# Lacing the block merges of a triangular inverse with pieces of three projections, with raw buffers of their own for the modulation weights and one transpose for the gathered diagonal blocks

## The chip, the cores and the metric

One Trainium2 chip, one core. The time is device microseconds of one execution of the whole program. Three runs of the kernel before gave 1310.15, 1297.49 and 1303.28 us, a median of 1303.28 us. The engines are called PE (matmul), DVE, ACT, POOL and SP (which issues the transfers).

## The reference, cut to what matters

Two layers (DEPTH 2) over 256 context tokens and 256 latent tokens of width 1024. Each layer has a token mixer and an MLP. The mixer has eight neighbourhood attention heads of width 64 and four gated DeltaNet heads of width 128, which run in both directions. In the DeltaNet heads the reference forms, for every chunk of 64 tokens,

```
a = where(strict, (kb @ k^T) * decay, 0)        # strictly lower triangular
tinv = unit_lower_inverse(a)                    # (I + a)^-1
u = tinv @ (v * beta) ;  w = tinv @ (kb * eg)
```

and then scans the chunks in order with `u`, `w` and the state. The attention heads need the projections `nq`, `nk`, `nv`, and the gated norm needs `z`; none of these depends on the inverse. The modulation vectors (six of width 1024 a layer, from `silu(c) @ w_ada`) are needed at the layer norms, at the end of the mixer and in the MLP.

## The kernel before, in words

All arithmetic is in fp32. A large weight block of 128 x 1024 is fetched by SP into a raw buffer (`wraw`, line 236, a ring of four), split by ACT into a rounded high part (`whi`, line 248) and by DVE into the rest (`wlo`, line 250); both rings have three buffers. A projection is eight steps over the contraction, each of three matmuls of 128 x 512 (`mm3`, lines 274 to 276), 24 in all; the function `getw` hands the weights out in a fixed list order, and up to three blocks are fetched ahead.

The program is written as one long stream, and a scheduler turns it into a queue for each engine: at each moment of its own simulated time it gives an engine the earliest written instruction that is ready there. It does not model the TensorE clock. Work written later fills gaps of work written earlier, as far as its data, its buffers and its PSUM banks allow. Inside a `manual_schedule` region the TensorE instructions of the region keep their written order among themselves; others may still be put between them.

The mixer of a layer (function `mixer`) goes as follows.

- Four DeltaNet heads (`gdn_head`), then the gates (`gates1`, `gates2`).
- For each of four token tiles t, the products `kk` (line 813), the decays (`decay`, ACT exponentials, line 805) and the product of both (line 816) fill 8 of the 32 matrices of 128 x 128 in `U`. Each matrix has four diagonal blocks of 32 x 32.
- The 128 diagonal blocks are inverted together on DVE: line 824 transposes them from `U` to `MT`, line 825 negates them into `Y`, 30 pairs of DVE operations (lines 831 and 833, here called the substitution) run over them, line 834 transposes the result to `MT`, line 836 spreads it over `XT` by four ACT copies, one for each quadrant of 32 partitions, and line 838 spreads its transpose over `U` by four DVE transposes.
- The merges, lines 841 to 872, put the blocks of 32 together to blocks of 64, and those to blocks of 128, in two halves `t2` of 16 matrices. Of each half: 32 matmuls `p1` (line 849), copies to `y1`, 64 matmuls `pz` (lines 853, 854), copies back into `U` and `XT`; then for each of two tiles 8 matmuls `p2` (line 862), a copy to `y2`, 8 matmuls `p3` (lines 867, 868) and the copies back.
- The scan over the chunks (`scan_step`, `o_stage`), written behind the merges.
- Behind that, the string of the layer after its X says in which order the remaining work is written (`run_order`): f is two steps of the modulation (`fill`; one step is one 512 KB block of `w_ada`, line 299, and four small matmuls, line 301), N, K, Q and Z are projections, a is an attention of two heads for one token tile (`attend`). The layer before the X has the heads H and the gates B and C. There are 32 steps of modulation weights and four closing steps in a mixer.

The modulation weights go through the same ring `wraw` as the large weights.

Of the kernel before, what the change touches and what calls it, by code (L numbers as in the profile page):

```python
# [11 lines left out]
F32 = mybir.dt.float32  # L12
# [3 lines left out]
AF = mybir.ActivationFunctionType  # L16
# [6 lines left out]
KT = 8  # L23
# [6 lines left out]
NEG = -1e30  # L30

NHOLD = 6
NB0 = 3
GATE = [("w1t", 0), ("w1", 1, 0)]
PARTS = 4
# [2 lines left out]
PAIR2 = True  # L38
KP_OUT = (2, 3, 0, 1)
CFG = {  # L40
    "ord0": "HHBHHCXfNffffNNfffffNKQffaaaKaQfaaKfaQfaffaaKfaQfaZaaaZZfffafffZ",
    "ord1": "BHHHHCNfffXNfffNfNfKfQfaafKfQfaaKfQKfaQfaafffZZZaZ", "tr": 7, "tr2": 2, "acc": 2, "g": 3, "n": 3,
    "late": 3, "tord": (0, 1, 2, 3), "adab": "n", "depth": 3, "npre": 8, "pre1": (0, 2, 3), "vt": "n",
    "tm": 1, "tmh": (2, 3), "gt": 2, "f02": 1, "f12": 2, "f13": 1,
    "start": "WLmmmWme01WLmmmm2eLmbm0mmbLe1m2m0mme12012bb", "cin": 7, "rows": 1,
# [131 lines left out]
def body(ctx, tc, a, out, dump=None):  # L177
# [289 lines left out]
    def mixer(l, hT, pre, ctx_m):  # L467
# [110 lines left out]
        nv = M.tile([128, 4, 8, 65], F32, name="nv", tag="nv")  # L578
        G.memset(nv[:, :, :, 64:65], 1.0)

        def proj_nv(hp):
            w = getw("w_vz", l, 0, hp)
            ps = proj_T(w, 0, "psv")
# [146 lines left out]

        biases = {}

        def proj_qk(hp, kind):
            if not kind:
                biases[hp] = load_bias(hp)
            w = getw("w_na", l, 2 * hp + kind)
            t0 = 256 if (last and kind) else 0
            ps = proj_T(w, t0, "psn")
# [28 lines left out]

        cnt2 = dict.fromkeys("NKQZaH", 0)

        def run_order(o):  # L770
            for c in o:
                if c in "fBC":
                    {"f": fill, "B": gates1, "C": gates2}[c]()
                    continue
                i = cnt2[c]
                cnt2[c] += 1
# [20 lines left out]
        def decay(t, d, form, bias):  # L797
# [8 lines left out]
                             scale=-1.0 if form == "c" else 1.0)  # L806
            return D_

        for t in ts:
# [10 lines left out]
        q4 = [slice(32 * b, 32 * b + 32) for b in range(4)]  # L820
        MY = M.tile([128, 2, 32, 32], F32, name="MY", tag="my")
        MT, Y = MY[:, 0], MY[:, 1]
# [18 lines left out]
        for t2 in range(2):  # L841
            n0 = 16 * t2
            y1 = tr("y1").rearrange("p (n c) -> p n c", n=16)
            p1 = sm("p1").rearrange("p (n c) -> p n c", n=16)
            pz = sm("pz").rearrange("p (n c) -> p n c", n=16)
            A_, B_ = [slice(64 * r, 64 * r + 32) for r in range(2)], [slice(64 * r + 32, 64 * r + 64) for r in range(2)]
            for r in range(2):
                for n in range(16):
                    PE.matmul(p1[B_[r], n], U[A_[r], n0 + n, B_[r]], XT[A_[r], n0 + n, A_[r]], start=True, stop=True)
                S.activation(y1[B_[r]], p1[B_[r]], AF.Copy)  # L850
            for r in range(2):
                for n in range(16):
                    PE.matmul(pz[A_[r], n], y1[B_[r], n], U[B_[r], n0 + n, B_[r]], start=True, stop=True)
                    PE.matmul(pz[B_[r], n], U[B_[r], n0 + n, B_[r]], y1[B_[r], n], start=True, stop=True)
                V.tensor_scalar(U[A_[r], n0:n0 + 16, B_[r]], pz[A_[r]], -1.0, None, op0=ALU.mult)
                S.activation(XT[B_[r], n0:n0 + 16, A_[r]], pz[B_[r]], AF.Copy, scale=-1.0)
            lo_, hi_ = slice(0, 64), slice(64, 128)
            for t in (2 * t2, 2 * t2 + 1):
                n0 = 8 * t
                p2 = sm("p2").rearrange("p (n c) -> p n c", n=8)  # L860
                for n in range(8):
                    PE.matmul(p2[hi_, n], U[lo_, n0 + n, hi_], XT[lo_, n0 + n, lo_], start=True, stop=True)
                y2 = tr("y2").rearrange("p (n c) -> p n c", n=8)
                S.activation(y2[hi_], p2[hi_], AF.Copy)
                p3 = sm("p3").rearrange("p (n c) -> p n c", n=8)
                for n in range(4):
                    PE.matmul(p3[lo_, n], y2[hi_, n], U[hi_, n0 + n, hi_], start=True, stop=True)
                    PE.matmul(p3[hi_, 4 + n], U[hi_, n0 + 4 + n, hi_], y2[hi_, 4 + n], start=True, stop=True)
                V.tensor_scalar(U[lo_, n0:n0 + 4, hi_], p3[lo_, 0:4], -1.0, None, op0=ALU.mult)
                S.activation(XT[hi_, n0 + 4:n0 + 8, lo_], p3[hi_, 4:8], AF.Copy, scale=-1.0)  # L870
                V.tensor_tensor(U[:, n0 + 4:n0 + 8], XT[:, n0 + 4:n0 + 8],
                                beta[:, t, 4:8].unsqueeze(2).to_broadcast([128, 4, 128]), op=ALU.mult)
        if l == 0:
            dump("LT", U)

        Sst = {t: XT[:, 8 * t:8 * t + 8].rearrange("p (d h) c -> p h d c", d=2) for t in ts}
        vn, on = {}, {}
# [89 lines left out]
        for step in range(4):  # L967
            for d in range(2):
                scan_step(step, d)
        obt = M.tile([128, 16, 2, 64], F32, name="ob", tag="my")  # L970
        run_order(post)
        while steps:
# [340 lines left out]
```

## Time and profile before

| what | before |
| --- | --- |
| median of three runs | 1303.28 us |
| the profiled execution | 1304.05 us, its span 1302.3 us |
| PE busy | 1234.8 us, 95% of the span |
| DVE busy | 875.1 us, 67% |
| ACT busy | 604.6 us, 46% |
| mean granted TensorE clock | 0.963 |
| bytes read from HBM | 187.46 MB, 146 GB/s |

PE is busy nearly all the time, but a busy PE is one that holds a matmul, at whichever clock it was granted. The mean clock of 0.963 therefore belongs to the reading: a stretch at 0.50 does half the work of a stretch at 1.00 while it looks as busy. Times in the sections below are microseconds from the start of the span; the first layer's mixer lies before 330, the second one's between 780 and 1060.

### The profile page before, as it was taken

How to read it: one execution, taken by the hardware profiler on the slowest of the kernel's cores; microseconds unless marked ns; L12 is line 12 of the kernel's file. 1: busy time of each engine (PE TensorE's matmuls, PEld its weight loads, DVE VectorE, ACT ScalarE, POOL GpSimd, SP SyncE). 2: the span in 40 equal slices, each digit the busy share in tenths (PEclk: the TensorE clock that was granted, in tenths of full speed). 3: DMA queues.
4: the chain of work that ended last, by engine and by line, in shares of the span. 5: the costliest groups of instructions: out<-in, count | busy, mean ns of one | idle time of the engine just before them, and what ended most of it. 6: DMA issues, size and time to landing. Idle time of an engine off the chain costs nothing.

```text
span 1302.3 us, 20475 instructions
## 1 busy us (share of the span) xinstructions
PE 1234.8 (95%) x7976; PEld 1006.3 (77%) x7976; DVE 875.1 (67%) x1681; ACT 604.6 (46%) x1079; POOL 81.6 (6%) x82
## 2 busy tenths in 40 slices
PE   7999998999999999999999999899979998999997
PEld 3676666988878988777788888675669877788996
DVE  3788695466579955344444488897965668866677
ACT  2554545565555732322322455555454655544552
POOL 0212100001001000000000001221000010000000
PEclk9999995899999999999999999999958999899999
DMA  9613661023255643533532256235720256555552
GB/s 329 213 65 102 211 219 46 17 78 117 79 194 182 225 150 109 165 130 115 164 129 99 97 178 204 72 107 191 235 92 14 85 179 231 199 184 191 186 187 98
DMA packets 62721, 190.93 MB, mean 147 GB/s; under 512 B 7808, under 2 KB 17824, under 8 KB 62624
## 3 DMA queue, kind: packets, MB, share of 16 engines
q1 hardware_dynamic: 62624, 189.62, 44.2%
q8 instruction: 63, 1.03, 0.3%
q14 instruction: 34, 0.28, 0.1%
HBM read 187.46 MB, written 2.13 MB: 146 GB/s over the span
## 4 chain that ended last, share of the span: by engine, by line
PE 71%; DVE 11%; ACT 4%; issue 2%; POOL 1%; DMA 1%; DVEq 0%; ACTq 0%; POOLq 0%
PE pst L274 7%; PE pst L276 7%; PE pst L275 7%; PE pm L274 7%; PE pm L276 7%; PE pm L275 7%; PE pss L716 3%; PE adaps L301 2%; DVE wlo L250 2%; PE pss L696 2%; PE pss L713 2%; PE psn L274 1%; PE psn L275 1%; PE psn L276 1%; ACT XT L836 1%
## 5 line engine op out<-in xcount | busy, mean ns | idle before, releaser
L250 DVE TENSOR_TENSOR wlo<-wraw,whi 128x1024 fp32r<-128x1024 f32 x224 | 274.7, 1228 | 184.7 <-ACT whi L248 184.3
L248 ACT ACTIVATE whi<-wraw 128x1024 fp32r<-128x1024 f32 x224 | 237.0, 1060 | 316.6 <-PE pst L276 168.9
L274 PE MATMUL pm<-hhi,whi 128*128 128x256 f32 (+1 forms) x544 | 176.4, 324 | 0.8 <-ACT whi L248 0.7
L276 PE MATMUL pm<-hhi,wlo 128*128 128x256 f32 (+1 forms) x544 | 174.5, 321 | 0.0
L275 PE MATMUL pm<-hlo,whi 128*128 128x256 f32 (+1 forms) x544 | 174.4, 321 | 0.0
L274 PE MATMUL pst<-whi,ah 128*128 128x512 f32 x384 | 150.0, 391 | 0.0
L275 PE MATMUL pst<-wlo,ah 128*128 128x512 f32 x384 | 149.5, 389 | 0.0
L276 PE MATMUL pst<-whi,al 128*128 128x512 f32 x384 | 149.1, 389 | 0.0
L274 PEld LDWEIGHTS pm<-hhi,whi 128*128 128x128 f32 x544 | 103.5, 190 | 14.4 <-issue 5.8
L276 PEld LDWEIGHTS pm<-hhi,wlo 128*128 128x128 f32 x544 | 103.6, 190 | 7.7
L275 PEld LDWEIGHTS pm<-hlo,whi 128*128 128x128 f32 x544 | 103.6, 190 | 7.3
L274 PEld LDWEIGHTS pst<-whi,ah 128*128 128x128 f32 x384 | 72.1, 188 | 15.6 <-issue 0.8
L276 PEld LDWEIGHTS pst<-whi,al 128*128 128x128 f32 x384 | 72.1, 188 | 14.8
L275 PEld LDWEIGHTS pst<-wlo,ah 128*128 128x128 f32 x384 | 72.1, 188 | 14.7
L274 PE MATMUL psg<-hhi,whi 128*128 128x512 f32 (+1 forms) x216 | 78.2, 363 | 4.6 <-ACT XT L529 2.3
L276 PE MATMUL psg<-hhi,wlo 128*128 128x512 f32 (+1 forms) x216 | 78.0, 362 | 0.2 <-DVE wlo L250 0.2
L275 PE MATMUL psg<-hlo,whi 128*128 128x512 f32 (+1 forms) x216 | 77.8, 361 | 0.0
L531 DVE SCALAR_TENSOR_TENSOR XT<-U,cw,XT 128x512 f32<-128x512 f32 (+1 forms) x96 | 66.9, 728 | 0.5 <-ACT XT L529 0.4
L1191 ACT ACTIVATE ah<-mr 128x256 fp32r<-128x256 f32 (+1 forms) x68 | 33.5, 492 | 65.6 <-DVE mr L1189 65.6
L301 PE MATMUL adaps<-wraw,scT 128*32 128x256 f32 x640 | 56.0, 397 | 4.8 <-DMA wraw<-w_ada 4.6
L229 POOL TENSOR_TENSOR rs<-ve,mh 128x1 f32<-128x1 f32 x12 | 12.5, 1044 | 629.3 <-DVE bmv L394 362.2
L1192 DVE TENSOR_TENSOR al<-mr,ah 128x256 fp32r<-128x256 f32 (+1 forms) x68 | 35.2, 518 | 24.3 <-ACT ah L1191 24.2
(659 smaller groups left out, 2467.4 us busy)
## 6 DMA issues: line engine op xcount, KB each, us to landing
wraw<-w SPq DMA_DIRECT2D x140, 512.0 KB
wraw<-w_ada SPq DMA_DIRECT2D x80, 512.0 KB
wraw<-w_gdn SPq DMA_DIRECT2D x27, 512.0 KB
wraw<-w_out SPq DMA_DIRECT2D x24, 512.0 KB
xa<-w_ada SPq DMA_DIRECT2D x32, 256.0 KB
wraw<-w_vz SPq DMA_DIRECT2D x16, 512.0 KB
wraw<-w_na SPq DMA_DIRECT2D x16, 512.0 KB
lnrow<-lnr SPq DMA_DIRECT2D x8, 512.0 KB
```

Source lines behind the costliest of these rows:

```text
L248: S.activation(hi, r, AF.Copy)
L250: V.tensor_tensor(lo, r, hi.bitcast(F32), op=ALU.subtract)
L274: PE.matmul(o, l[0], r[0], start=start, stop=False)
L275: PE.matmul(o, l[0], r[1], start=False, stop=False)
L276: last_mm[:] = [PE.matmul(o, l[1], r[0], start=False, stop=stop).ins]
L301: PE.matmul(st["ps"][32 * g:32 * g + 32, :256], scT[:, k, :], w[:, 256 * g:256 * g + 256], start=(k == 0), stop=(k == 7), tile_position=(0 ...
L531: V.scalar_tensor_tensor(av, cin[:, sg:, kk:kk + 256], cw[:, b, kk:kk + 1], av, op0=ALU.mult, op1=ALU.add)
L696: PE.matmul(ps[:, :128 * nkt], nqT[hp][:, a2, qs], nkT[hp][i][:, a2, :128 * nkt], start=i == 0, stop=i == 1)
L713: PE.transpose(ps[:, 128 * kt_:128 * kt_ + 128], p_[:, 128 * kt_:128 * kt_ + 128], ident)
L716: PE.matmul(ps[:, 0:65], p_[:, 128 * kt_:128 * kt_ + 128], nv[:, kt_, hd], start=kt_ == 0, stop=kt_ == nkt - 1)
L1191: S.activation(ah, r, AF.Copy)
L1192: V.tensor_tensor(al, r, ah.bitcast(F32), op=ALU.subtract)
```

## The change

Four edits.

1. Modulation weights no longer use the ring `wraw`; they have two buffers of their own (`wada`).
2. The diagonal blocks are gathered into `Y` by four ACT copies of 32 partitions x 256 elements as soon as a tile's part of `U` is there, and all are transposed by one DVE transpose of 128 x 1024. After the substitution, the second result is transposed by one DVE transpose into `MT` as well, and spread over `U` by two ACT copies and two DVE copies of 32 x 1024.
3. The merges become a function `merge(work)`. Its TensorE instructions are in one `manual_schedule` region. `p1` and `pz` use two PSUM banks each, and their matmuls alternate between the two 64-row halves r. After each of the four stages of each half `t2`, three contraction steps (nine matmuls) of a projection are written; the eight pieces make up three projections.
4. The strings: the letter Y runs the merges laced with the projections of the next three letters, S runs the scan. Work written behind the X and ahead of Y is now ahead of the merges and the scan in the stream.

```
-    "ord0": "HHBHHCXfNffffNNfffffNKQffaaaKaQfaaKfaQfaffaaKfaQfaZaaaZZfffafffZ",
-    "ord1": "BHHHHCNfffXNfffNfNfKfQfaafKfQfaaKfQKfaQfaafffZZZaZ", ...
+    "ord0": "HHBHHCXfNffNffNffKffYQNKSffffffaaaaQfaaKfaQfaffaaKfaQfaZaaaZZfffafffZ",
+    "ord1": "BHHHHCNfffXNffNffKffQfYNKQSfffaaffaafKfQKfaQfaafffZZZaZ", ...
...
-            w = wraw(a["w_ada"][l, 128 * k:128 * (k + 1), 1024 * n:1024 * (n + 1)])
+            w = P0.tile([128, 1024], F32, name="wada", tag="wada", bufs=2)
+            SP.dma_start(w, a["w_ada"][l, 128 * k:128 * (k + 1), 1024 * n:1024 * (n + 1)])
...
+        def dense(o):
+            end = None
+            for c in o:
+                ...
+                for k in range(KT):
+                    mm3(ps[:, t0:], (w[0][:, 128 * k:128 * k + 128], w[1][:, 128 * k:128 * k + 128]),
+                        (hT[0][:, k, t0:], hT[1][:, k, t0:]), k == 0, k == KT - 1)
+                    if k == LACE - 1 and end:
+                        end()
+                    yield
+                end = ...
+            end()
...
+            for b in range(4):
+                S.activation(Y[q4[b], :, 8 * t:8 * t + 8].rearrange("p i n -> p n i"), U[q4[b], 8 * t:8 * t + 8, q4[b]], AF.Copy)
...
-        for b in range(4):
-            V.transpose(MT[q4[b]], U[q4[b], :, q4[b]].rearrange("p n i -> p i n"))
+        V.transpose(MT, Y)
...
+        V.transpose(MT, Y)
         for b in range(4):
-            V.transpose(U[q4[b], :, q4[b]].rearrange("p n i -> p i n"), Y[q4[b]])
+            o, i = U[q4[b], :, q4[b]].rearrange("p n i -> p i n"), MT[q4[b]]
+            V.tensor_copy(o, i) if b % 2 else S.activation(o, i, AF.Copy)
...
+        def merge(work):
+            def chunk():
+                for _ in range(LACE):
+                    next(work, None)
+            ...
+            with tc.manual_schedule(engines={nc.tensor.engine}):
+                for t2 in range(2):
+                    ...
+                    p1 = [sm("p1").rearrange("p (n c) -> p n c", n=16) for _ in range(2)]
+                    for n in range(16):
+                        for r in range(2):
+                            PE.matmul(p1[r][B_[r], n], U[A_[r], n0 + n, B_[r]], XT[A_[r], n0 + n, A_[r]], start=True, stop=True)
+                    for r in range(2):
+                        S.activation(y1[B_[r]], p1[r][B_[r]], AF.Copy)
+                    chunk()
+                    ... # pz, chunk(), p2 of both tiles, chunk(), p3 of both tiles, chunk()
```

## Rows read from the trace of the kernel before

**Rows 1.** Windows (stretch: us, engines busy (instructions), granted clock, DMA share, GB/s).

```profile
160.30:193.80 33.50, 31.03 (x187) 21.84 (x187) 31.42 (x82) 12.29 (x20) 0.00 (x0) 1.00 0.67 226
193.80:206.00 12.20, 7.28 (x86) 4.76 (x85) 11.54 (x9) 11.09 (x9) 0.00 (x0) 0.71 0.34 117
206.00:242.00 36.00, 36.00 (x512) 30.50 (x510) 13.36 (x35) 13.37 (x28) 0.00 (x0) 0.58 0.06 16
242.00:320.00 78.00, 77.30 (x590) 66.18 (x590) 48.89 (x145) 48.51 (x138) 8.58 (x6) 1.00 0.24 74
...
944.70:956.00 11.30, 3.76 (x69) 2.66 (x68) 11.14 (x9) 10.43 (x9) 0.00 (x0) 0.73 0.48 164
956.00:993.00 37.00, 37.00 (x542) 31.97 (x540) 15.96 (x39) 14.95 (x31) 1.83 (x1) 0.62 0.09 27
```

**Rows 2.** Waits of PE (line, waited for: us in total, times, longest).

```profile
PE p L849 <- ACT y L850: 8.7, 2, 5.3
PE adaps L301 <- DMA wraw<-w_ada: 4.6, 5, 1.6
```

**Rows 3.** Timeline of DVE, first layer (start us, us, line, out<-in, count).

```profile
150.97 8.09 DVE L824 STREAM_TRANSPOSE MY<-U 32x1024 f32<-32x1024 f32 x4
...
193.80 2.10 DVE L834 STREAM_TRANSPOSE MY<-MY 128x1024 f32<-128x1024 f32 x1
195.82 7.72 DVE L838 STREAM_TRANSPOSE U<-MY 32x1024 f32<-32x1024 f32 x4
```

**Rows 4.** Timeline of ACT, first layer.

```profile
195.99 7.85 ACT L836 ACTIVATE XT<-MY 32x1024 f32<-32x1024 f32 x4 [0.98 <-DVE MY L834]
...
220.21 0.37 ACT L870 ACTIVATE XT<-p 64x256 f32<-64x256 f32 x1
```

**Rows 5.** Groups of DVE by line, 160 to 194 (count, busy us, mean ns, idle).

```profile
L833 DVE TENSOR_TENSOR MY<-MY,btmp 128x30 f32<-128x30 f32 (+14 forms) x30 | 9.9, 330 | 0.8
...
L250 DVE TENSOR_TENSOR wlo<-wraw,whi 128x1024 fp32r<-128x1024 f32 x5 | 6.1, 1219 | 0.1
```

**Rows 6.** Timeline of PE, first layer.

```profile
100.06 0.39 PE L275 MATMUL psg<-hlo,whi 128*128 128x512 f32 x1
100.29 0.39 PE L276 MATMUL psg<-hhi,wlo 128*128 128x512 f32 x1
...
206.09 0.24 PE L853 MATMUL pz<-U,y 32*32 32x32 f32 x1
206.10 0.24 PE L854 MATMUL pz<-y,U 32*32 32x32 f32 x1
206.12 0.24 PE L849 MATMUL p<-XT,U 32*32 32x32 f32 x1
206.14 0.24 PE L853 MATMUL pz<-U,y 32*32 32x32 f32 x1
...
213.00 1.97 PE L862 MATMUL p<-XT,U 64*64 64x64 f32 x16
...
243.02 1.00 PE L716 MATMUL pss<-nv,p__2505 128*128 128x65 f32 x8
```

**Rows 7.** Groups of PE by line, 117.7 to 196.

```profile
L301 PE MATMUL adaps<-wraw,scT 128*32 128x256 f32 x165 | 14.4, 387 | 1.7 <-DMA wraw<-w_ada 1.7
...
L274 PE MATMUL psv<-hhi,whi 128*128 128x512 f32 x32 | 12.9, 405 | 0.0
L274 PE MATMUL psn<-hhi,whi 128*128 128x512 f32 x32 | 12.8, 401 | 0.2 <-PE adaps L301 0.2
```

**Rows 8.** Groups of PE by line, 196 to 242.

```profile
L274 PE MATMUL psn<-hhi,whi 128*128 128x512 f32 x6 | 3.9, 644 | 0.0
L696 PE MATMUL pss<-KS,QS 128*128 128x512 f32 (+1 forms) x6 | 3.7, 608 | 0.0
```

**Rows 9.** Groups of PE by line, second layer, 946.5 to 994.6.

```profile
L696 PE MATMUL pss<-KS,QS 128*128 128x512 f32 x5 | 3.5, 693 | 0.0
...
L274 PE MATMUL psn<-hhi,whi 128*128 128x512 f32 x4 | 2.7, 669 | 0.0
```

**Rows 10.** Windows within the merges of the first layer.

```profile
232.00:234.00 2.00, 2.00 (x25) 1.68 (x25) 1.25 (x4) 0.69 (x2) 0.00 (x0) 0.72 0.00 0
234.00:236.00 2.00, 2.00 (x77) 1.89 (x69) 0.84 (x2) 0.51 (x1) 0.00 (x0) 1.00 0.03 8
236.00:238.00 2.00, 2.00 (x7) 1.39 (x7) 0.81 (x5) 1.93 (x4) 0.00 (x0) 0.63 0.00 0
```

More of the change, by code (lines that the diff above doesn't have):

```diff
@@ L32 @@
 NHOLD = 6
+LACE = 3
+NLACE = 3
 NB0 = 3
@@ L768, in mixer @@
         cnt2 = dict.fromkeys("NKQZaH", 0)
+        def dense(o):
+            end = None
+            for c in o:
+                i = cnt2[c]
+                cnt2[c] += 1
+                w = getw(*(("w_vz", l, 0, i) if c == "N" else ("w_na", l, 2 * i + "KQ".index(c))))
+                ps = acc("psv" if c == "N" else "psn")
+                t0 = 256 if last and c == "Q" else 0
+                for k in range(KT):
[4 more added lines that the diff above has]
+                    yield
+                end = (lambda i=i, ps=ps: proj_nv(i, ps)) if c == "N" else (lambda i=i, c=c, ps=ps: proj_qk(i, "KQ".index(c), ps))
+            end()
         def run_order(o):
+            o = iter(o)
             for c in o:
-                if c in "fBC":
-                    {"f": fill, "B": gates1, "C": gates2}[c]()
+                if c == "Y":
+                    merge(dense([next(o) for _ in range(NLACE)]))
+                    continue
+                if c in "fBCS":
+                    {"f": fill, "B": gates1, "C": gates2, "S": lambda: scan()}[c]()
                     continue
@@ L807, in decay @@
             return D_
+        q4 = [slice(32 * b, 32 * b + 32) for b in range(4)]
+        MY = M.tile([128, 2, 32, 32], F32, name="MY", tag="my")
+        MT, Y = MY[:, 0], MY[:, 1]
         for t in ts:
@@ L873, in mixer @@
-        if l == 0:
-            dump("LT", U)
+        def merge(work):
+            def chunk():
+                for _ in range(LACE):
+                    next(work, None)
+            A_, B_ = [slice(64 * r, 64 * r + 32) for r in range(2)], [slice(64 * r + 32, 64 * r + 64) for r in range(2)]
+            lo_, hi_ = slice(0, 64), slice(64, 128)
+            with tc.manual_schedule(engines={nc.tensor.engine}):
+                for t2 in range(2):
+                    n0 = 16 * t2
+                    y1 = tr("y1").rearrange("p (n c) -> p n c", n=16)
+                    p1 = [sm("p1").rearrange("p (n c) -> p n c", n=16) for _ in range(2)]
[5 more added lines that the diff above has]
+                    chunk()
+                    pz = [sm("pz").rearrange("p (n c) -> p n c", n=16) for _ in range(2)]
+                    for n in range(16):
+                        for r in range(2):
+                            PE.matmul(pz[r][A_[r], n], y1[B_[r], n], U[B_[r], n0 + n, B_[r]], start=True, stop=True)
+                            PE.matmul(pz[r][B_[r], n], U[B_[r], n0 + n, B_[r]], y1[B_[r], n], start=True, stop=True)
+                    for r in range(2):
+                        V.tensor_scalar(U[A_[r], n0:n0 + 16, B_[r]], pz[r][A_[r]], -1.0, None, op0=ALU.mult)
+                        S.activation(XT[B_[r], n0:n0 + 16, A_[r]], pz[r][B_[r]], AF.Copy, scale=-1.0)
+                    chunk()
+                    tt, y2 = (2 * t2, 2 * t2 + 1), {}
+                    for t in tt:
+                        n0 = 8 * t
+                        p2 = sm("p2").rearrange("p (n c) -> p n c", n=8)
+                        for n in range(8):
+                            PE.matmul(p2[hi_, n], U[lo_, n0 + n, hi_], XT[lo_, n0 + n, lo_], start=True, stop=True)
+                        y2[t] = tr("y2").rearrange("p (n c) -> p n c", n=8)
+                        S.activation(y2[t][hi_], p2[hi_], AF.Copy)
+                    chunk()
+                    for t in tt:
+                        n0 = 8 * t
+                        p3 = sm("p3").rearrange("p (n c) -> p n c", n=8)
+                        for n in range(4):
+                            PE.matmul(p3[lo_, n], y2[t][hi_, n], U[hi_, n0 + n, hi_], start=True, stop=True)
+                            PE.matmul(p3[hi_, 4 + n], U[hi_, n0 + 4 + n, hi_], y2[t][hi_, 4 + n], start=True, stop=True)
+                        V.tensor_scalar(U[lo_, n0:n0 + 4, hi_], p3[lo_, 0:4], -1.0, None, op0=ALU.mult)
+                        S.activation(XT[hi_, n0 + 4:n0 + 8, lo_], p3[hi_, 4:8], AF.Copy, scale=-1.0)
+                        V.tensor_tensor(U[:, n0 + 4:n0 + 8], XT[:, n0 + 4:n0 + 8],
+                                        beta[:, t, 4:8].unsqueeze(2).to_broadcast([128, 4, 128]), op=ALU.mult)
+                    chunk()
+                for _ in work:
+                    pass
+            if l == 0:
+                dump("LT", U)
@@ L965, in o_final, with scan @@
             to_mix(of, 4, 4, t)
-        for step in range(4):
-            for d in range(2):
-                scan_step(step, d)
+        def scan():
+            for step in range(4):
+                for d in range(2):
+                    scan_step(step, d)
         obt = M.tile([128, 16, 2, 64], F32, name="ob", tag="my")
```

47 lines of the change are left out of this document (7 added, 40 removed).

## The prediction

> **What bounds the kernel now.** The page's table of engines comes first: PE is busy 95% of the span, so a gain must come out of PE's remaining idle time, out of stretches in which it is busy at half clock, or out of work that PE no longer does. The windows around the inverse show both kinds of loss [rows 1]. In the substitution (160.3 to 193.8) DVE is busy 31.4 of 33.5 us and PE 31.0, on projections and modulation steps that fill in. Between 193.8 and 206.0 PE has 7.3 us of work in 12.2. [...] The second layer repeats it: 3.8 us of work in 11.3, then 37.0 us at 0.62. The waits of PE name what stood before the merges: `p1` waits 8.7 us in two places for the copy to `y1` [rows 2], which stood on ACT behind the four copies into `XT` [rows 4]. So a layer loses about 5 to 7.5 us of idling and, as 36 us at 0.58 do 21 us of work, about 15 us by the clock: some 40 us in both layers are the most that this change can attack.
>
> **The change part by part.** Times are those of the profiled execution, 1304.05 us, 0.8 us above the median of the runs.
>
> *Gather.* Out go four DVE transposes, 8.1 us, between the last product and the negation [rows 3]. In come four ACT copies of 32 x 256 and one transpose of 128 x 1024, for which line 834 has 2.1 us [rows 3]. A copy lies between 0.37 us (64 x 256, contiguous) and a quarter of line 836's 1.96 us, so 0.49 [rows 4]; I take 0.49, as both scatter with a stride. 4 x 0.49 + 2.1 = 4.1, which is 4.0 us less. The twelve copies of the first three tiles (5.9 us) fall between the decays on ACT, which DVE and the last tile wait for; ACT's gaps hide only part. I take 2 us back: 2 us gained, ends 0 and 4.
>
> *Substitution.* Its own DVE work is 2 x 9.9 = 19.8 us of 33.5 [rows 1, 5]; the rest is weight splits (five, 6.1 us [rows 5]) and other work of projections. Fewer projections are now written ahead of the merges (in the first layer four behind the X, instead of everything), and some splits fit beside the ACT gather. I take 6 us off in the first layer, 4 in the second, where one projection more stays ahead; ends 0 and 11 (about all but the splits of four weights).
>
> *Spreading the results: a new wait.* The second transpose writes `MT`, which the four `XT` copies read, so on DVE it waits 7.85 us for them [rows 4], with splits queued behind it; ACT's two copies into `U` wait for it, with the `y1` copies near them, and `pz` waits for the diagonal blocks in `U`. From the end of the substitution to `pz`: 2.1 + 7.85 + 2.1 + two DVE copies. A copy of 32 x 1024 lies between 1.22 (the two-input pass over 1024 contiguous elements [rows 5]) and 1.93 (line 838 a quadrant [rows 3]), and I take the latter for its stride: 15.9 us, against 12.2 before [rows 1]. That is 3.7 us lost, at least 2.3. `pz` then starts at 206 - 2 - 6 + 3.7, near 202, in the first layer, and some 2.5 us earlier in the second. [...]
>
> *Merges.* Dense matmuls start 0.23 us apart at full clock [rows 6], so a piece of nine takes 2.1 us. Three streams of 32 x 32 records each advance every 0.05 us at half clock (206.09 to 206.14) [rows 6], so alternating the halves r lets 64 records of `p1` or 128 of `pz` pass in about 1.7 us at half and 0.85 at full clock (a matmul is two records). `p2` of a tile (16 records) takes about 1.8 us at half clock [rows 6], so 1.7 us for two tiles at full; `p3`, two streams of 8, half of it. From the first `pz` to the end: 2 x 0.85 + 0.85 + 2 x 1.7 + 2 x 0.85 = 7.7 us of merges and seven pieces, 14.5 us, together 22; with 3 us for copies that a piece doesn't cover, 25 us, against 36 and 37 [rows 1]. The first piece lies in the wait before `pz`. So the scan can start 11 + 4 = 15 us earlier in either layer.
>
> *What is owed.* PE is full behind the merges (242 to 320) [rows 1], so work not done by then costs its time later. First layer, before: 4 projections N and (32 + 6)/8 = 4.75 of K and Q by 242 [rows 7, 8]; after: 3 + 1 ahead and 3 laced, 7. Owed 1.75 x 24 x 0.23 = 9.7 us. Six attention heads ran in 196 to 242 [rows 8]; none can any more, because Q0 is in the lace. At two dense matmuls and up to twelve short ones of 0.125 us (the stretch from 243.02) [rows 6] a latent head takes 2 us, a context one half; 8 us for the six. Against it, modulation steps fill PE while it waits: 165 records, 21 steps, had run by 196 [rows 7], and with buffers of their own the other 11 can come ahead, at 0.5 to 0.7 us each: 6 us paid. Owed 11.7, so the first layer gains 3. Second layer: owed half a projection, 2.7 us, and five heads, 10 us [rows 9]; four of these heads have K0, Q0 and N0 ahead of the lace and may run early, I count half, 4 us, and 4 us for modulation: owed 5, so the gain is 10.
>
> *Own buffers.* The number of transfers on SP stays. PE's waits for modulation weights, 4.6 us [rows 2], lie in the same stretches and are in the sum above. SP's queue is in order, so a modulation block that waits for its two buffers holds up weights behind it; both ends, 5 us gained or lost. POOL has nothing new.
>
> Sum: 1304 - 3 - 10 = 1291 us.
>
> **Rivals.**
>
> *Slower: the lace runs at half clock.* Ahead of the lace PE loses three to four projections of filling, some 20 us a layer, so it reaches the merges after idling. For it: the clock went from 1.00 to 0.63 right after two microseconds of short matmuls, though dense ones had gone before [rows 10]. Against it: the scan's mix of 128-wide matmuls holds 1.00 for 78 us [rows 1]. It decides when the clock has not risen after the second piece. The 22 us from `pz` become 44, so the layers come to +19 and +12: 1335 us; at half clock for half of the lace, 1313. [...] Chance 0.2.
>
> *The waste only moves.* The gain at the scan is paid back in idling before the lace: if the modulation steps don't come ahead (10 us more owed in both layers) and no head runs early (4 us), the sum is 1305. For it: DVE, not PE, sets the length of the substitution. Chance 0.2.
>
> *More.* Without splits among it the substitution needs little more than its 20 us, so 5 us a layer further, and the heads in the second layer all run early, 4 us: 1277. For it: PE at 0.60 and less between 193.8 and 206 leaves room; the buffers freed from the ring bring modulation steps into the DeltaNet heads' gaps. Chance 0.25.
>
> **How the numbers follow.** The forecast has 0.35, with 1279 to 1303 of its own (the ends of the gather, the copies and the substitution). The runs spread about half a per cent either way, so 1% is what this kernel's measurement can tell from no change: below 1290 is faster, above 1316 slower. Faster: just under half of the forecast and nearly all of "more", 0.41. Slower: most of the half-clock rival, with a little of the rest, 0.18. Within: 0.41. The range 1272 to 1318 takes in both neighbours and the milder form of the slow rival.
>
> **What would show it.** Right: the clock at 1.00 within two pieces of the lace, the lace some 25 us, `pz` near 202, PE emptier between 165 and 195, the scan from about 227 and 978, heads and projections later. Wrong: a clock of 0.5 through the lace; a substitution still 33 us long; the second transpose late; a gap in the scan because SP brought modulation weights ahead of projections.

## The result, and the profile after

The changed kernel takes 1322.05 us (median of four runs, 1321.36 to 1326.68), the kernel before beside it 1301.44 us: a ratio of 1.0153, 95% interval 1.0112 to 1.0194. That is 1.5% slower, 31 us above the forecast of 1291 us and 4 us above its range. The profiled execution took 1321.36 us, its span is 1319.6 us, PE is busy 1216.5 us of it (92%, before 95%), and the mean granted clock is 0.966 (before 0.963).

The windows around the inverse, with the columns of [rows 1] (stretch: us, then PE, weight loads, DVE, ACT, POOL busy with counts, granted clock, DMA share, GB/s): the substitution, the spreading, the lace, the scan, and the spreading and the lace of the second layer.

```profile
159.90:187.10 27.20, 7.83 (x55) 3.58 (x47) 24.01 (x69) 3.31 (x5) 0.00 (x0) 0.63 0.40 121
187.10:201.00 13.90, 6.31 (x77) 4.79 (x77) 5.26 (x4) 11.67 (x8) 0.00 (x0) 0.50 0.01 1
201.00:228.00 27.00, 26.42 (x516) 21.35 (x515) 10.70 (x16) 13.03 (x21) 0.00 (x0) 0.98 0.13 41
228.00:306.00 78.00, 77.46 (x583) 61.44 (x582) 45.98 (x127) 43.81 (x125) 4.03 (x4) 1.00 0.39 123
...
955.80:969.70 13.90, 8.28 (x93) 5.07 (x92) 5.65 (x5) 11.73 (x8) 0.00 (x0) 0.50 0.35 110
969.70:994.00 24.30, 24.30 (x520) 20.49 (x520) 10.22 (x19) 12.63 (x20) 0.00 (x0) 0.99 0.14 46
```

Two things are to be seen. The lace does what it was written for: 27 us at 0.98 and 24 us at 0.99, where the merges took 36 and 37 us at 0.58 and 0.62 [rows 1]. But in the substitution PE is busy 7.83 of 27.2 us, where it was busy 31.03 of 33.5. The waits of PE in 140 to 240 us name the place: it stands in front of the first merge matmuls until the copies into `XT` are done, once for 17.3 us; before, its longest wait there was 5.3 us [rows 2].

```profile
PE p L883 <- ACT XT L861: 20.8, 2, 17.3
PE adaps L304 <- DMA wada<-w_ada: 4.0, 2, 2.2
```

What the milestones make of it, first matmul of the first layer's scan, first matmul of its MLP's second product, first matmul of the second layer's scan, in the timeline of PE after:

```profile
228.23 1.05 PE L941 MATMUL pvn<-vtok,U 128*128 128x128 f32 x8
...
479.80 0.40 PE L276 MATMUL pst<-whi,ah 128*128 128x512 f32 x1
...
994.09 1.06 PE L941 MATMUL pvn<-vtok,U 128*128 128x128 f32 x8
```

and before:

```profile
242.03 1.16 PE L896 MATMUL pvn<-vtok,U 128*128 128x128 f32 x8
...
467.71 0.40 PE L274 MATMUL pst<-whi,ah 128*128 128x512 f32 x1
...
991.18 1.16 PE L896 MATMUL pvn<-vtok,U 128*128 128x128 f32 x8
```

The first scan starts 13.8 us earlier, and yet the layer ends 12.1 us later: 25.9 us were owed. Measured from that later end, the second scan starts 12.1 - 2.9 = 9.2 us earlier, and the program ends 17.3 us later: 9.2 + 17.3 - 12.1 = 14.4 us owed.

**An account of PE's time.** Windows of 5 us over a whole span, the last one cut at its end, give PE's idle time (length less busy time) and what the clock cost (busy time x (1 - granted clock)). What is left is taken as work at full clock; it lies between 1189 and 1204 us in all kernels of this study. So a span is that work, plus idle time, plus clock loss. Before: 1194.9 + 67.5 + 40.0 = 1302.4; after: 1197.1 + 103.1 + 19.4 = 1319.6. The change won 20.6 us from the clock and lost 35.6 to idling, of which 25 (5 to 30) between 120 and 200 us and some 13 between 900 and 1000 us. The table of the experiments gives these columns for every run.

The clock column is the rougher one. It takes a stretch at 0.50 to do half the work. That is near for dense matmuls, which start 0.43 us apart at 0.50 (196.8 to 201.0 in the changed kernel) and 0.23 at 1.00. But the alternating `pz` gets through four matmul records every 0.054 us at 0.50 and every 0.033 at 1.00 (201.0 to 202.5), so in the merges the column says too much. A difference of clock loss is read here for its direction; its size can be off by the 15 us in which the work differs.

### The profile page after: what moved, and what is told of

Same layout as the page of the kernel before. It is cut to its first block, busy times and chain, and to the rows that moved or that the text cites. A ratio compares the mean times of both kernels' runs of the same rounds, so it can differ in the third digit from the quotient of the medians.

```text
span 1319.6 us, 20473 instructions
## 1 busy us (share of the span) xinstructions
PE 1216.5 (92%) x7976; PEld 979.6 (74%) x7976; DVE 854.4 (65%) x1673; ACT 630.3 (48%) x1115; POOL 82.3 (6%) x82
## 4 chain that ended last, share of the span: by engine, by line
PE 72%; DVE 12%; ACT 6%; issue 2%; POOL 2%; DMA 2%; SPq 0%; DVEq 0%; ACTq 0%; POOLq 0%
PE pst L276 7%; PE pst L278 7%; PE pst L277 7%; PE pm L276 7%; PE pm L278 6%; PE pm L277 6%; PE pss L719 3%; PE adaps L304 3%; PE psn L276 2%; DVE wlo L252 2%; PE psn L277 2%; PE psn L278 2%; PE pss L699 1%; PE pss L716 1%; DVE XT L534 1%
## 5 line engine op out<-in xcount | busy, mean ns | idle before, releaser
L276 PEld LDWEIGHTS pm<-hhi,whi 128*128 128x128 f32 x544 | 103.6, 190 | 14.4 <-issue 5.8
L304 PE MATMUL adaps<-wada,scT 128*32 128x256 f32 x640 | 62.9, 420 | 18.3 <-DMA wada<-w_ada 18.3
L304 PEld LDWEIGHTS adaps<-wada,scT 128*32 128x32 f32 x640 | 16.3, 112 | 48.0 <-DMA wada<-w_ada 27.7
L276 PE MATMUL psn<-hhi,whi 128*128 128x512 f32 (+1 forms) x128 | 51.2, 400 | 0.8 <-DVE KL L758 0.8
```

Source lines behind the costliest of these rows:

```text
L276: PE.matmul(o, l[0], r[0], start=start, stop=False)
```

## The experiments

Each is an edit of the changed kernel or of the kernel before. Ratios are to the kernel before on the same chip, whose median there lay between 1298.59 and 1305.98 us, so medians of different chips compare to some 7 us at worst. Idle time and clock loss are of the profiled execution, in us, as above. (The expectation for e18 has 67 us of idle time for e3, as it counts the last window beyond the end of the span.)

| kernel | median us | ratio, 95% | idle (in 120 to 200) | clock loss |
| --- | --- | --- | --- | --- |
| before | 1301.44 | | 67 (5) | 40 |
| changed | 1322.05 | 1.0153, 1.0112 to 1.0194 | 103 (30) | 19 |
| e1 own buffers alone | 1310.19 | 1.0035, 1.0009 to 1.0061 | 65 (5) | 41 |
| e2 gather alone | 1305.63 | 1.0008, 0.9980 to 1.0036 | 64 (6) | 44 |
| e3 unlaced | 1282.89 | 0.9833, 0.9796 to 0.9870 | 65 (6) | 10 |
| e4 lace, ring for modulation | 1321.96 | 1.0132, 1.0096 to 1.0168 | 108 (34) | 19 |
| e5 new merges alone | 1292.88 | 0.9938, 0.9909 to 0.9967 | 67 (6) | 35 |
| e6 lace, POOL's queue | 1339.49 | 1.0300, 1.0260 to 1.0339 | 116 (34) | 23 |
| e7 later projections laced | 1313.94 | 1.0107, 1.0070 to 1.0145 | 84 (13) | 31 |
| e8 lace of one | 1323.91 | 1.0185, 1.0147 to 1.0223 | 102 (31) | 21 |
| e9 lace of one, own bank | 1341.98 | 1.0291, 1.0258 to 1.0324 | 95 (7) | 40 |
| e10 unlaced, ring | 1292.41 | 0.9895, 0.9851 to 0.9939 | 67 (4) | 34 |
| e11 unlaced, old gather | 1288.85 | 0.9894, 0.9855 to 0.9932 | 63 (5) | 24 |
| e12 unlaced, halves in turn | 1303.39 | 0.9993, 0.9967 to 1.0019 | 64 (6) | 41 |
| e13 lace emptied in place | 1299.63 | 0.9964, 0.9932 to 0.9997 | 70 (6) | 22 |
| e14 modulation written ahead | 1315.38 | 1.0079, 1.0048 to 1.0109 | 95 (22) | 27 |
| e15 unlaced, two banks | 1298.73 | 0.9961, 0.9932 to 0.9990 | 75 (7) | 24 |
| e16 lace of one, last | 1317.98 | 1.0107, 1.0073 to 1.0142 | 98 (25) | 16 |
| e17 the same, other rings | 1309.75 | 1.0065, 1.0039 to 1.0092 | 85 (15) | 30 |
| e18 unlaced, four slots | 1294.19 | 0.9955, 0.9924 to 0.9985 | 70 (6) | 32 |

**Edits 1 and 2 alone, and edit 1 undone.** e1: on the kernel before, `w = wraw(...)` becomes the two lines with `wada`. e2: on the kernel before, the gather and the spreading of the changed kernel. e4: on the changed kernel, `wraw` again.

> The kernel before with edit 1 alone (modulation blocks in two buffers of their own). Theory 'cover' (the loss of the changed kernel is TensorE idling ahead of the lace, because the lace has taken the projections that filled the substitution, and the modulation steps that could replace them are held up): the projections are still free to fill, so within 6 us of before, 1295 to 1307. Theory 'gather' (ACT copies among the decays and the wait of the second transpose make the loss): the same as before. Theory 'two buffers' (modulation steps with two buffers of their own come too late, whatever is laced): 8 us or more slower, 1309 or above.

> The kernel before with edit 2 alone (gather by ACT copies, one transpose before and after the substitution, spreading by two ACT and two DVE copies). 'Gather': 8 to 20 us slower than before, since the last product comes some 3 us later after an earlier start of the chain and pz waits for the second transpose, in either layer. 'Cover': within 5 us of before, because PE is filled by projections all this time. 'Two buffers': the same as before.

> The changed kernel with edit 1 undone (modulation blocks through the ring of four again). 'Two buffers': 8 us or more faster than the changed kernel, 1313 or below. 'Cover': 1316 to 1328, since the ring is then filled with the weights of the lace and the modulation steps stop ahead of it just the same. 'Gather': the same as the changed kernel.

Own buffers cost 0.35% alone and nothing under the lace; the gather alone is worth nothing. (The 1310 of e1 is over the bound that was set for 'cover' and over the 1309 of 'two buffers', because the kernel before was at 1305.71 beside it; 4.5 us over that is within the 6 of 'cover' and short of the 8 of 'two buffers'.) 'Gather' and 'two buffers' fall. The loss is in edit 3 or 4.

**Without the lace.** e3: the strings of the kernel before, with merges and scan first behind the X, and nothing in the pieces. e13: the changed strings, the three letters moved behind the scan.

```
-                    merge(dense([next(o) for _ in range(NLACE)]))
+                    merge(iter(()))
e3   "ord0": "HHBHHCXYSfNffffNNfffffNKQff...   "ord1": "BHHHHCNfffXYSNfffNfNfKfQf...
e13  "ord0": "...XfNffNffNffKffYSNQKffffff...   "ord1": "...XNffNffKffQfYSNKQfff...
```

> The changed kernel without the lace: merges with alternating halves and two banks stand first behind the X, then the scan, then everything else in the order of the kernel before; edits 1 and 2 stay. 'Cover': the loss of 20 us is gone, 1303 or below, with PE busy over 28 of 33 us during the substitution and the clock near 0.6 in the merges again. 'Gather' and 'two buffers': at least two thirds of the loss stays, 1315 or above.

> The changed kernel with its own strings, the merges at the same place in the written order and the three projections directly behind merges and scan, but nothing laced. Theory 'handed out in order' (a laced projection takes its bank and weight slots at its place in the written order, so nothing dense written behind it starts earlier): the three projections come ahead by themselves, idle TensorE time between 120 and 200 falls from 30 to 10 us or less, 1278 to 1292. Theory 'strings' (what was written ahead of the merges and behind them is the loss, laced or not): 1308 or above.

e3 is 1.7% faster than before, e13 0.4%; in both the idle time ahead of the merges is back at 6 us. 'Cover' had that right and the clock wrong: it expected 0.6 in the merges of e3 again. e13 differs from the changed kernel by the lace alone, and the clock loss is about the same (22 and 19 us): the lace costs 22 us by the medians, and it costs them in idling. e13 lies above its range, and 17 us above e3; 11 us more of clock loss go with that (its profiled execution, 1292.41 us, is among its fastest). The changed strings bring nothing by themselves. The `psn` matmuls of projections K and Q in 165 to 200 us (columns: PE, weight loads, DVE, ACT of these tiles) in the changed kernel

```profile
165.00:200.00 35.00, 3.16 (x8) 2.49 (x9) 2.74 (x4) 2.35 (x4) 0.54 0.23 73
```

and in e13, where the three projections stand behind merges and scan in the written order and come ahead by themselves:

```profile
165.00:200.00 35.00, 21.71 (x87) 15.87 (x87) 7.55 (x11) 6.49 (x11) 1.00 0.62 198
```

In e3 the merges run near full clock with no lace (two windows, one of each layer, around the merges):

```profile
200.00:240.00 40.00, 36.43 (x648) 28.91 (x649) 23.38 (x54) 34.03 (x56) 1.63 (x1) 0.96 0.17 54
950.00:1000.00 50.00, 49.79 (x728) 43.34 (x727) 33.42 (x96) 33.05 (x72) 3.63 (x2) 0.98 0.15 46
```

The scheduler puts dense matmuls and attention between the merges of its own accord.

**What shuts the other work out.** First the number of laced projections and which ones: e8 laces N3 alone (`NLACE = 1`, strings `...KffYNSQK...` and `...QfYNSKQ...`); e7 has the changed kernel's three ahead and laces the next three (`...NffKffNQKffYQKQS...`, `...QfNKQYKQKS...`).

> The changed kernel with one projection (N3) in the lace instead of three; the other two are written behind the scan, so that they may run ahead when their weights, slots and banks are free. 'Bound projections': two of the three weight slots are free for projections in front of the merges, so most of the loss goes, 1285 to 1305. 'Queue': the blocked queue loosens too, so the same. 'Lace': about a third of the way from the changed kernel to the unlaced one stays as loss, near 1296, with the cost in the merges and not ahead of them.

> The changed kernel with other projections in the lace: the three that it laced (N3, Q0, K1 and in the second layer N3, K1, Q1 or their like) are written ahead of the merges again, and the three after those in the list are laced. 'Bound projections': TensorE is busy over 25 of the 33 us of the substitution again, and the time falls to 1280 to 1300. 'Queue': the queue is blocked as before, so 1312 or above. A third theory, 'lace' (pieces bound in order between the merges cost by themselves, wherever they come from): 1305 or above though the substitution is covered.

e8, which none of the three theories had above 1305, refutes the simple form of 'bound projections': one laced projection, two free weight slots, and the same loss. From 165 to 200 no projection K or Q runs at all:

```profile
165.00:200.00 35.00, 0.00 (x0) 0.00 (x0) 2.75 (x4) 2.12 (x4) 0.54 0.22 70
```

So what is laced holds back what is written behind it, though that is ready. e7 fills most of the gap (13 us idle) and is still 15 us slower than before, nearer to 'lace' than to 'bound projections'; its time alone would also fit 'queue', which e6 answers below. The theory that came of it: every ring (PSUM banks, weight slots, scratch buffers) hands out its places in the written order, so that a projection tied to the lace keeps its place in each ring it uses, and all later users of that ring wait with it. e9 takes the accumulator of N3 out of the ring:

```
-                ps = acc("psv" if c == "N" else "psn")
+                ps = PP.tile([128, 512], F32, name=..., tag="lace", bufs=1)     # and "n": 2 in place of 3
```

> The lace of one projection (N3) again, but N3 accumulates in a PSUM bank of its own, taken from the ring of the modulation and the attention (two banks there in place of three); all else as in the lace of one. Theory 'handed out in order' (a ring's banks are given to projections in the order in which they are written, so no projection written behind the lace can start before the lace's first piece): now the two projections behind it start before the merges, TensorE is busy over 20 of the 33 us of the substitution, and the time falls below 1312. Theory 'region' (the lace's own TensorE order, not the bank, shuts the others out): TensorE idles from 173 to 190 as in the lace of one, 1318 or above.

```profile
165.00:200.00 35.00, 30.00 (x125) 22.61 (x123) 8.25 (x12) 7.10 (x12) 1.00 0.39 128
```

125 dense matmuls in place of none, and the idle time ahead of the merges falls from 31 to 7 us: for the accumulators the theory is shown. But the time, expected below 1312, rises to 1342. Its control, e15 (e3 with `"n": 2`), lies between its two ranges; the third bank given up costs 16 us there by itself:

> The unlaced kernel with two in place of three banks for modulation and attention: the control for the lace of one with a bank of its own, 1342. If the missing third bank made that kernel slow: 1300 or above. If not, within 6 us of the unlaced kernel, 1277 to 1289, and the lace of one costs in another place though its cover is back.

The other 43 us between e9 and e15 come with the lace, as idling and clock loss from 200 us on (40 + 32 us in 200 to 400 and 950 to 1100, against 18 + 11 in e15), and are not taken apart further. e16 keeps all banks and writes Q0 and K1 ahead (`...KffQKYNS...`); e17 adds one edit, the bank of N3's transposes and the buffer of its copy:

```
-            vT = tr2("vT")
+            vT = (tr if own else tr2)("vT")          # own: this N is laced
-            pv_ = {"n": sn, "g": sm, "a": acc}[CFG["vt"]]("pvt")
+            pv_ = (acc if own else {"n": sn, "g": sm, "a": acc}[CFG["vt"]])("pvt")
```

> The lace of one projection, with the other two (Q0 and K1) written ahead of the merges in place of behind the scan. 'Handed out in order': 48 dense matmuls, 11 us, fill part of the 20 us in which TensorE idled, so idle time between 120 and 200 falls from 31 to about 20 and the time to 1308 to 1316. 'Region' or 'a lace costs by itself': 1318 or above.

> The lace of one projection, last (Q0 and K1 ahead of it), with one edit: the laced N3 takes the bank for its transposes and the buffer for its copy from rings that the attention doesn't use. 'Handed out in order', for the rings behind the projection too: attention heads and new groups of modulation steps written behind the lace can now start ahead of it, so idle time between 120 and 200 falls from 25 to 15 or less, and the time by 5 to 15 us from 1318, to 1303 to 1313. 'Dense work alone matters' (only the accumulators and weight slots count): 1314 to 1322 with the idle time unchanged.

The matmuls of the modulation steps (`adaps`) in 173 to 200 us, e16 and then e17. A step has four matmuls, and each stands as two records in the trace (640 records for 80 blocks), so eight records are a step:

```profile
173.00:200.00 27.00, 0.00 (x0) 0.00 (x0) 0.34 (x1) 0.00 (x0) 0.67 0.23 75
```

```profile
173.00:200.00 27.00, 7.56 (x64) 1.63 (x64) 0.85 (x2) 0.00 (x0) 0.71 0.69 220
```

e16 is 2 us above its range, at the bound of 'region', with 25 us idle in place of 20: behind Q0 and K1 nothing else came. In e17 eight modulation steps come ahead, once what follows the laced projection no longer holds a place in the rings of the attention and the modulation; the idle time falls from 25 to 15 us and the time by 8, as expected. Attention heads come ahead in the second layer, three by 960 us where e16 has none; in the first there are none by 200 in either. The theory holds for these rings too (bank and buffer were changed together), and since the region is the same in both kernels, 'region' falls. The rings of raw buffers and weight slots were not tried by themselves.

**The modulation steps and SP's queue.** In the changed kernel SP stood with a dense weight ahead of the modulation blocks; the timeline of SP (start, us, line, transfers):

```profile
167.83 3.61 SPq L302 DMA_DIRECT2D wada<-w_ada  x2
173.89 46.69 SPq L238 DMA_DIRECT2D wraw<-w_na  x3
229.91 0.80 SPq L302 DMA_DIRECT2D wada<-w_ada  x2
```

Three weights take 46.69 us to be issued: SP waits 45.6 us for raw buffers that the splits on DVE (line 252) have yet to free; the splits come at 209, 219 and 229, between the pieces of the lace, whose matmuls free the slots for them (ACT's half of these splits, line 250, waited 0.76, 2.95 and 1.25 us for matmuls of `psn` and `psv`). No modulation block is issued from 174 to 229.91. e6 gives the modulation blocks POOL's queue (`G.dma_start`), e14 writes 12 and 6 more steps ahead of the lace (`...KffffffffYNQKSaaaa...`, `...QffffYNKQSaa...`).

> The changed kernel with the modulation blocks issued by POOL instead of SP, so that no dense weight stands ahead of them in the same queue. Theory 'queue' (TensorE idles ahead of the lace because the modulation steps are shut out by SP's blocked queue): the idle time of 165 to 195 is filled by modulation steps, 10 us or more faster than the changed kernel, 1312 or below. Theory 'bound projections' (it idles because the next three projections are tied to the lace, and those behind them to their weight slots and banks): two buffers let at most a block each 2 us through, 0.57 us of TensorE work each, so within 8 us of the changed kernel, 1314 to 1326.

> The changed kernel with 12 modulation steps of the first layer and six of the second moved in the strings from behind the scan to ahead of the lace. If the loss is that modulation steps did not come ahead (the credit of 6 and 4 us in the prediction): a step is 0.57 us of TensorE and a block needs some 2 us of the queue, so the 20 us before the lace hold some ten steps; 4 to 10 us faster than the changed kernel, 1312 to 1318, with idle time between 120 and 200 down to 25 or less. If the transfers are bound by other waits of the queue: 1319 to 1327.

With a queue of its own (e6) only one step runs in that time, so the queue wasn't what shut them out in the first layer:

```profile
173.00:200.00 27.00, 1.08 (x8) 0.20 (x8) 0.42 (x1) 0.00 (x0) 0.50 0.17 57
```

Over the whole span POOL stood 519.7 us in front of these issues until PE had run a step and freed its buffer:

```profile
L302 POOL DMA_DIRECT2D wada<-w_ada x80 | 43.6, 545 | 542.5 <-PE adaps L304 519.7 <-DMA wada<-w_ada 12.7 <-PE pss L716 4.3
```

The changed kernel shows the same without any edit: two blocks issued before 174 lay in their two buffers until PE ran both steps behind the lace,

```profile
229.21 1.07 PE L304 MATMUL adaps<-wada,scT 128*32 128x256 f32 x16
```

Neither theory of e6 had the time, 17 us above the changed kernel; why POOL's queue is that much worse was not pursued. Written ahead (e14), nine steps run in the same stretch:

```profile
173.00:200.00 27.00, 9.72 (x72) 1.84 (x72) 0.66 (x2) 0.00 (x0) 0.50 0.74 228
```

and the time is 6.7 us lower, as expected. So modulation steps that did not come ahead are worth at least 7 us of the loss; PE was still idle for 12.6 of the 27 us of that stretch.

**What the clock needs in the merges.** e5 is the kernel before with the new merges alone, e10 and e11 are e3 with edit 1 or edit 2 undone, e12 is e3 with `for r in range(2)` outside `for n in range(16)` in `p1` and `pz`, e18 is e10 with four slots for split weights.

> The kernel before with nothing but the new merges (halves alternated, two banks each for p1 and pz, p2 and p3 of two tiles together, written in one manual region ahead of everything else behind the X); no lace, edits 1 and 2 undone. Theory 'merges' (the 23 us that the unlaced kernel is ahead of before come from the merges alone, which run at full clock with the scheduler's own dense work between them): 1276 to 1286, the merges from the first pz to the scan some 25 us long at a clock near 1.00. Theory 'shorter chain' (the gather and the single transposes bring the merges forward, and that is the gain): 1295 or above.

> The unlaced kernel (new merges, new gather, no lace) with edit 1 undone, so that modulation blocks share the ring of four again. Theory 'clock' (the unlaced kernel gains by merges at full clock, which hangs on TensorE being busy right before and within them): 1277 to 1290 if the merges of both layers keep the clock, near 1293 if the first layer's fall to half clock as in the kernel with the new merges alone. Theory 'own buffers help when nothing is laced': 1287 or above with the clock as in the unlaced kernel.

> The unlaced kernel with edit 2 undone: four transposes gather and four spread again, edit 1 and the new merges stay. 'Clock': the time follows the granted clock in the merges alone, 1280 to 1287 where both layers' merges run near 1.00, 1291 to 1298 where one layer's run at half. 'Gather' (the new gather and spreading are worth something by themselves once the lace is gone): 1288 or above with the clock as in the unlaced kernel.

> The unlaced kernel with the two 64-row halves of p1 and pz one after the other again in place of alternating; two banks each and the one region stay. 'Clock': 64 records of p1 and 128 of pz take longer by at most 1 us each at full clock, four bursts a layer, so within 6 us of the unlaced kernel, 1278 to 1292, as long as the clock holds. 'Alternation' (what keeps the clock is that the halves alternate): the merges fall to half clock, 1295 or above.

> A candidate: the unlaced kernel with modulation back in the ring of four, and the room that this frees given to a fourth slot for split weights. If a fourth slot lets one more weight be ready while TensorE is at its fullest, idle time falls below the 67 us of the unlaced kernel and the time to 1270 to 1282; if weights are early enough already, 1280 to 1294, by the clock in the merges.

The windows of e5 and then of e12, to be read against those of e3:

```profile
200.00:240.00 40.00, 36.95 (x563) 31.24 (x564) 18.49 (x41) 18.02 (x30) 0.00 (x0) 0.53 0.13 40
950.00:1000.00 50.00, 44.34 (x724) 39.31 (x725) 31.70 (x81) 32.38 (x64) 3.63 (x2) 0.90 0.14 48
```

```profile
200.00:240.00 40.00, 37.63 (x576) 31.11 (x578) 17.27 (x36) 25.37 (x34) 0.00 (x0) 0.70 0.12 41
950.00:1000.00 50.00, 44.80 (x607) 37.71 (x606) 22.84 (x51) 30.12 (x42) 1.82 (x1) 0.67 0.19 61
```

e12 is at 0.70 and 0.67 and as fast as before, as 'alternation' had it: with the halves in turn the unlaced kernel's gain is gone. Alternating is not enough, though: e5 alternates, has its first layer at 0.53, and lies between the ranges of its two theories, 7 us above that of 'merges'. In e10 (0.91 and 0.66), e11 (0.88 and 0.83) and e18 (0.96 and 0.59) these windows are also partly at half clock. The profiled executions of e10 and e11 are 15.0 and 3.8 us longer than that of e3, with 23 and 14 us more of clock loss and 2 us more and 1 us less of idle time. So the clock goes the way of the times, though not in their size, and idling doesn't set them apart. The fourth slot of e18 saved no idle time. The runs of e5, e10, e11 and e18 spread over 9 to 15 us each (e10: 1281.79 to 1296.53), those of e3 over 4. What decides over the clock in a layer is left open, and with it what the own buffers and the gather are worth in the unlaced kernel. The best version found is e3, 1282.89 us, faster than both kernels.

## Why the prediction was wrong, step by step

- **Merges at full clock: right.** The matmuls of the first `pz` fell from 0.24 to 0.19 us at 202.1, and the granted clock was 1.00 in 202.2 to 204.0 and in 203.0 to 228.2; from first `pz` to scan 27 us (forecast 25), scan at 228.2 (227). The half-clock rival is refuted. In the first layer only the first piece, behind the waits of 17.3 and 3.6 us and `p1`, ran at 0.50, with 0.43 us a matmul (196.8 to 201.0).
- **Substitution: right.** 27.2 us against 33.5, 6.3 less (forecast 6); in the second layer 27.8 against 34.7, 6.9 less (forecast 4).
- **Spreading: the wait right, the length too long.** The second transpose waited 7.90 us, as forecast. From the end of the substitution to `pz` it took 13.9 us, not 15.9: 1.7 us lost against before, less than the "at least 2.3". That `pz` came at 200.98, near the 202 of the forecast, is luck: this term was 2.0 us too long, and the next one 1.6 us too good. Its rows, DVE and then ACT:

```profile
156.71 1.25 DVE L849 STREAM_TRANSPOSE MY<-MY 128x1024 f32<-128x1024 f32 x1 [1.24 <-ACT MY L845]
...
187.13 1.91 DVE L859 STREAM_TRANSPOSE MY<-MY 128x1024 f32<-128x1024 f32 x1
...
196.93 1.25 DVE L862 STREAM_TRANSPOSE MY<-MY 128x1024 f32<-128x1024 f32 x1 [7.90 <-ACT XT L861]
198.21 2.15 DVE L865 COPY U<-MY 32x1024 f32<-32x1024 f32 x2
```

```profile
142.50 2.66 ACT L845 ACTIVATE MY<-U 32x256 f32<-32x256 f32 x4
...
189.13 7.77 ACT L861 ACTIVATE XT<-MY 32x1024 f32<-32x1024 f32 x4 [19.18 <-DVE MY L859]
```

  A DVE copy took 1.08 us (two in 2.15): less than the 1.93 taken, and below the 1.22 at the lower end of the forecast.
- **Gather: mis-sized.** The ACT copies take 0.66 us each, not 0.49, and hold up the decays behind them: from the first product in `U` to the end of the last it takes 19.5 us (134.5 to 154.0), before 12.7 (138.2 to 150.9). The transpose takes 1.25 us in place of 2.1. From the first product to the substitution it is 25.4 us against 22.1, 3.3 lost where 2 were to be gained; the substitution starts 0.4 us earlier only because the first product came 3.7 us earlier, which no term of the sum had. In the second layer the same stretch is 24.7 us against 20.5, 4.2 lost. In the kernel before this costs nothing in the whole (e2).
- **Own buffers: inside the bound of 5 us**: 4.5 us lost in e1, nothing in e4.
- **What is owed: the step that failed.** The forecast had 11.7 us in the first layer and 5 in the second; 25.9 and 14.4 were measured, 24 us more. The rest of the miss of 30 us is the scan, which started 13.8 + 9.2 us earlier, not 30; the gather, 11.5 us worse than forecast in both layers, is more than that. What PE had done by the first matmul of the scan shows which terms failed. First layer, before (100 to 242.03) and after (100 to 228.23); eight records are a projection (lines with hhi,whi) or a modulation step (`adaps`), one is a head (`pss`):

```profile
L301 PE MATMUL adaps<-wraw,scT 128*32 128x256 f32 x192 | 17.2, 405 | 1.7 <-DMA wraw<-w_ada 1.7
...
L274 PE MATMUL psn<-hhi,whi 128*128 128x512 f32 x38 | 16.7, 440 | 0.2 <-PE adaps L301 0.2
...
L274 PE MATMUL psv<-hhi,whi 128*128 128x512 f32 x32 | 12.9, 405 | 0.0
...
L696 PE MATMUL pss<-KS,QS 128*128 128x512 f32 x4 | 2.7, 664 | 0.0
...
L696 PE MATMUL pss<-KS,QS 128*128 128x256 f32 x4 | 1.7, 416 | 0.1
```

```profile
L276 PE MATMUL psv<-hhi,whi 128*128 128x512 f32 x32 | 13.5, 421 | 0.0
...
L304 PE MATMUL adaps<-wada,scT 128*32 128x256 f32 x128 | 12.7, 419 | 4.0 <-DMA wada<-w_ada 4.0
...
L276 PE MATMUL psn<-hhi,whi 128*128 128x512 f32 x24 | 11.3, 470 | 0.0
```

  The projections are as forecast, 7 after 8.75. The modulation is not: 16 steps after 24, where all 32 were to be done. So 8 steps were owed in place of a credit of 6 us. And 8 heads were owed, not 6, four latent and four context ones; by the forecast's own price (2 us and half of that) they cost 12 us, and its six alone 10, not 8. An estimate from these counts and prices, with 0.5 to 0.7 us a step, is 9.7 + 12 + 4 to 6 = 26 to 27 us, against the 25.9 measured. In the second layer (780 to 991.18 before, 780 to 994.09 after) half a projection and five of seven heads were owed, and the modulation was even, 24 steps in both: 2.7 + 10 = 13 us, against 14.4. Neither the 4 us for heads that run early nor the 4 us for modulation came:

```profile
L301 PE MATMUL adaps<-wraw,scT 128*32 128x256 f32 x192 | 15.0, 389 | 3.0 <-DMA wraw<-w_ada 2.9
...
L696 PE MATMUL pss<-KS,QS 128*128 128x512 f32 x7 | 4.3, 609 | 0.0
```

```profile
L304 PE MATMUL adaps<-wada,scT 128*32 128x256 f32 x192 | 19.1, 471 | 13.2 <-DMA wada<-w_ada 13.2
...
L699 PE MATMUL pss<-KS,QS 128*128 128x512 f32 x2 | 0.8, 391 | 0.0
```

- **Why the credits failed.** The forecast let modulation steps come ahead "with buffers of their own". The runs showed that what is tied to the lace keeps its place in every ring, and work written behind it can't pass, whichever buffers it has (e8; shown for the accumulators by e9, for the rings of the modulation and the attention by e17). PE, which was to be "emptier between 165 and 195", did nothing at all from 173.8 to 191.1.
- The rival "the waste only moves" named the right condition, that neither modulation steps nor heads come ahead, but priced it at 14 us. It counted the steps that ran ahead of the scan before as done, of which 8 fell behind as well, and it kept the price of six heads.
- **A premise behind the change, though no term of the sum,** was that a lace is needed for the clock; the expectation for e3 still has it. e3 has its merges near full clock (0.96 and 0.98) without one. In that kernel the alternating halves were needed for it, as with the halves in turn (e12) the same windows were at 0.70 and 0.67; that the work which the scheduler puts between them helps is argued, not shown.

## What to carry to other kernels

Before tying work into a chain by hand, list each ring that it takes a place in (accumulators, weight slots, scratch of what follows it): where places are handed out in the written order, everything behind it in any of these rings is tied too, and the cover of the stage before is gone. Account for a span as work at full clock plus idle time plus clock loss, window by window; a gain in one column can be paid for in another, as here 21 us for 36. When a chain of small matmuls loses the clock, first let its independent halves alternate and leave the filling to the scheduler: here the windows around the merges (200 to 240 and 950 to 1000 us) were at 0.54 and 0.66 before and at 0.96 and 0.98 in e3; the clock was won back in part in e5 (0.53 and 0.90), e10 (0.91 and 0.66), e11 (0.88 and 0.83) and e18 (0.96 and 0.59).

## What was not expected of the hardware

- PE stayed at half clock (0.50) for 38 us (204 to 242 in e5) while it was busy 37.08 us of them (508 records); in the changed kernel the clock rose at 202.1, after 7.1 us of work without a gap: `p1`, nine dense matmuls and 1.1 us of alternating `pz`. In e5 being busy did not by itself bring the clock back.
- A DVE transpose of 128 x 1024 took 1.25 us from contiguous input (lines 849 and 862) and 1.91 us from input read with a stride (line 859); a copy of 32 x 1024 into a strided output took 1.08 us on DVE and 1.98 us on ACT (two in 3.95).
